# Stage 0 of a two-layer encoder trunk: radix-4 step, gate and convolution silu on PSUM operands, and GpSimd's squares behind the first product

## The chip, the cores and the metric

The kernel runs on one core of one Trainium2 chip. The core has five engines with a queue each: TensorE (PE in the profile, its weight loads PEld), VectorE (DVE), ScalarE (ACT), GpSimd (POOL) and SyncE (SP), which issues most DMAs. The metric is the device time of one execution in microseconds, as the median of several runs; lower is better. SBUF is the working memory; PSUM is the memory that matmuls write, in 8 banks of 128 partitions by 512 float32 values.

## The reference

The input x is (1, 1024, 1024) in float32: sequence by model width. Layer 0 normalizes, makes one input projection, sends 512 of its columns through mixer A (a real 2-D Fourier transform over sequence and head, then a map for each head) and 2 × 512 through mixer B (a gated convolution over 31 taps, a layer norm for each head, silu), joins both in an output projection and adds x. Layer 1 uses a pooling mixer. Each layer ends in a SwiGLU feed-forward block.

```python
h = rmsnorm(x, norm_mix_g[layer])
p = h @ w_in_ab[e]
ya = fnet_heads(p[..., :A_WIDTH], fnet_map[e])          # fft2 over sequence and head, real part, map
yb = conformer_conv_heads(p[..., A_WIDTH:A_WIDTH + B_WIDTH], p[..., A_WIDTH + B_WIDTH:], ...)
y = jnp.concatenate([ya, yb], axis=-1) @ w_out_ab[e]
x = x + y
h = rmsnorm(x, norm_ffn_g[layer])
x = x + (silu(h @ w_gate) * (h @ w_up)) @ w_down

# conformer_conv_heads
u = v * sigmoid(gate)
u = conv31(u) + conv_b
yb = silu(layernorm_per_head(u))
```

## The kernel before, in words

**Data and number format.** Everything is held transposed: channels on the 128 partitions, the sequence of 1024 along the free dimension, in two halves of 512 (`HALVES`). Each float32 operand of a matmul is split into a rounded high part and a low part (the residue), and a product is three matmuls (`mm3`, L101 to L103: high by high, high by low, low by high). `split` (L88, L89) makes the parts: a cast on ACT, then a subtraction on DVE or POOL.

**The order of work.** The source lists the work in one order. The framework's planner fixes the order on each engine when the program is built, by its own estimates of durations and by the source's order as priority, and it gives out buffers in that plan. So ACT's squares stand between casts that the source lists ahead of them. On the chip each engine then works through its queue strictly in that order. Buffers belong to tags with a fixed number of slots: `ps` has 4 PSUM banks, `lnp` has 2, `acc` is a pair of banks, `half` has 6 slots in SBUF. A product that finds no free `ps` bank waits for the instruction that reads the old one last.

**Pacing.** `mm3` keeps marks: after each three matmuls the number of columns that PE has streamed so far. `paced(ins, rows)` makes an instruction wait for the first mark at or over `rows`.

**The start.** Two weight tiles (value and gate columns of the first convolution head) and x arrive by DMA. `split_x` (L163, L164) makes high and low parts `gxh`, `gxl` of x times the norm's gain for each of 8 channel tiles and a half. `in_mm` forms a product of 8 `mm3` for 128 output columns and one half. The norm's sum of squares is shared: POOL squares tiles 0, 2, 4, 6 (`sq_pool`, L172 to L176), ACT squares the other four and DVE adds them (L131, L134, L135). `inv_x` adds the two sums (L187), a matmul with a constant matrix (L140) sums over channels, and `rsqrt2` (L123 to L126) makes the factor `invs[t]` that multiplies products when they are evacuated.

**The gate.** `vg_evac` (L214 to L217) evacuates the value product and the gate product with the factor into SBUF tiles `vt` and `g`, applies the sigmoid on ACT in place, and writes their product to `us[c]`, the input of the convolution.

**The convolution in the background.** Its 31 taps for each of 4 channel tiles run beside the products: tiles 1 and 2 on DVE (L313, L315, accumulating in the PSUM pair `acc`), tile 0 on ACT and POOL (L304 multiplies into `pr`, L305 adds), tile 3 on both (L330 on DVE). `tick(used)` is called after each product: it counts the columns that PE streamed since the last call, turns them into microseconds, subtracts `used` for the DVE work of that product, and emits as many steps of DVE's convolution stream as fit; POOL's taps are paced by columns. `conv_ln` (L343 to L355) is the layer norm over a head's 128 channels, with two matmuls, and the silu (L354), whose result is split (L88, L89).

**The radix-4 step.** For each of 4 Fourier heads, two products are evacuated into a tile `at` of 1024 columns (L426). A radix-4 butterfly on its four quarters q0 to q3 follows (L434 to L439): q0 + q2, q1 + q3, q0 − q2, q1 − q3, then the sum and the difference of the first two. `split` makes `zh`, `zl` of the tile (L440). Then `fnet1` (two `ps` banks a step, evacuated at L462 and L463) and `fnet2` (one bank, L482 and L483) run for 8 steps, followed by the output projection's Fourier half (`op_one`, L504), its convolution half, and the feed-forward blocks.

Of the kernel before, what the change touches and what calls it, by code (L numbers as in the profile page):

```python
# [12 lines left out]
AF = mybir.ActivationFunctionType  # L13
ALU = mybir.AluOpType
# [5 lines left out]
KD = D // P  # L20
FF = 2816
NF = FF // P
TH = 512
TAPS = 31
PAD = TAPS // 2
# [10 lines left out]
HALVES = (slice(0, TH), slice(TH, S))  # L36

V_MIX, V_FFN, V_FIN, V_CB, V_LG, V_LB, V_PS = 0, 16, 32, 40, 44, 48, 52
# [4 lines left out]
def trunk(ctx: ExitStack, tc: tile.TileContext, xT, vecs, cw, w_in, w_out, fmap, pmap,  # L43
          wg, wu, wd, wdq, wdp, cen_m, pcnt, dft_h, dft_l, seq_h, seq_l, out):
    nc = tc.nc
# [6 lines left out]
    def big(name, dt=F32, cols=1024):  # L52
        return arena.tile([P, WW], dt, tag="big", name=name, bufs=28)[:, :cols]

    def half(name, dt=F32):
        return arena.tile([P, TH], dt, tag="half", name=name, bufs=HALF_BUFS)

    def small(name, dt=F32):
        return arena.tile([P, TH], dt, tag="ln", name=name, bufs=4)

    def bank(tag="ps"):
        return psum.tile([P, TH], F32, tag=tag, name=tag, bufs=4 if tag == "ps" else 2)

    TT = nc.vector.tensor_tensor
# [3 lines left out]
    vec = const.tile([P, NV], F32, name="vec")  # L68
# [18 lines left out]
    def split(hi, lo, src, eng=None):  # L87
        nc.scalar.copy(hi, src)  # L88
        (eng or nc.vector).tensor_tensor(out=lo, in0=src, in1=hi.bitcast(F32), op=ALU.subtract)  # L89
# [3 lines left out]
    def paced(ins, rows):  # L93

        mark = next((m for n, m in marks if n >= rows), marks[-1][1])
        tc.add_manual_dep(ins.ins, mark.ins.name, mybir.DependencyInfo(
            mybir.DependencyClass.Sync, mybir.DependencyReason.DATA), reason="pace")

    def mm3(ps, lhs, rhs, start, stop, **kw):
        (lh, ll), (rh, rl) = lhs, rhs  # L100
        nc.tensor.matmul(ps, lh, rh, start=start, stop=False, **kw)  # L101
        nc.tensor.matmul(ps, lh, rl, start=False, stop=False, **kw)  # L102
        mm = nc.tensor.matmul(ps, ll, rh, start=False, stop=stop, **kw)  # L103
        marks.append((marks[-1][0] + 3 * ps.free_size(), mm))
# [13 lines left out]
    def wslice(w, i):  # L118
        return w[0][:, i * P:(i + 1) * P], w[1][:, i * P:(i + 1) * P]

    def rsqrt2(ps, e, y, v):

        nc.scalar.activation(y, ps, AF.Abs_reciprocal_sqrt, bias=eps[:, e:e + 1])  # L123
        STT(out=v, in0=ps, scalar=(RMS_EPS, LN_EPS)[e], in1=y, op0=ALU.add, op1=ALU.mult)
        TT(out=v, in0=v, in1=y, op=ALU.mult)
        STT(out=v, in0=v, scalar=-3.0, in1=y, op0=ALU.add, op1=ALU.mult)  # L126
        return v
# [25 lines left out]
    xin = [big(f"xin{k}") for k in range(KD)]  # L153
# [6 lines left out]
    def split_x(t, k):  # L160
        hs = HALVES[t]
        g = gneg[:, V_MIX + k:V_MIX + k + 1]
        nc.scalar.activation(gx_h[k][:, hs], xin[k][:, hs], AF.Copy, scale=g)  # L163
        STT(out=gx_l[k][:, hs], in0=xin[k][:, hs], scalar=g, in1=gx_h[k][:, hs].bitcast(F32),  # L164
            op0=ALU.mult, op1=ALU.subtract)

    def sq_pool(t, pooled):
        hs = HALVES[t]
        accp = half("accp")
        for k in pooled:  # L170
            if k == pooled[0]:
                nc.gpsimd.tensor_tensor(out=accp, in0=xin[k][:, hs], in1=xin[k][:, hs], op=ALU.mult)  # L172
            else:
                pr = arena.tile([P, TH], F32, tag="pr", name="pr", bufs=2)
                nc.gpsimd.tensor_tensor(out=pr, in0=xin[k][:, hs], in1=xin[k][:, hs], op=ALU.mult)
                nc.gpsimd.tensor_tensor(out=accp, in0=accp, in1=pr, op=ALU.add)  # L176
        return accp

    def sq_rest(t, pooled):
        acc = half("acc")  # L180
        rest = [k for k in range(KD) if k not in pooled]
        for k in rest:
            sq_acc(acc, xin[k][:, HALVES[t]], k == rest[0])
        return acc

    def inv_x(acc, accp):
        TT(out=acc, in0=acc, in1=accp, op=ALU.add)  # L187
        return inv_from(acc)

    def in_w(m, **kw):  # L190
        return load_w(w_in[m], **kw)

    def in_mm(w, t, ps=None):
        ps = bank() if ps is None else ps
        for k in range(KD):
            mm3(ps, wslice(w, k), (gx_h[k][:, HALVES[t]], gx_l[k][:, HALVES[t]]), k == 0, k == KD - 1)
        return ps

    invs = [None, None]
    us = [big(f"u{c}", cols=UW) for c in range(4)]  # L200
# [9 lines left out]
        vg_evac(c, t, in_mm(wv, t, pv), in_mm(wgt, t, pg))  # L210

    def vg_evac(c, t, pv, pg):
        vt, g = half("vt"), half("g")
        TT(out=vt, in0=pv, in1=invs[t], op=ALU.mult)  # L214
        TT(out=g, in0=pg, in1=invs[t], op=ALU.mult)
        nc.scalar.activation(g, g, AF.Sigmoid)
        TT(out=us[c][:, PAD + t * TH:PAD + (t + 1) * TH], in0=vt, in1=g, op=ALU.mult)  # L217

    def make_tables():

# [27 lines left out]
    for k in range(KD):  # L248
        if k % 4 == 0:
            hs = HALVES[k // 4]  # L250
# [5 lines left out]
    pv, pg = [in_mm(wv, 0)], [in_mm(wgt, 0)]  # L256
# [4 lines left out]
    df_h, df_l = df_hl[:, 0:2 * P], df_hl[:, 2 * P:4 * P]  # L261
    for dst, src in ((df_h, dft_h), (df_l, dft_l)):
        paced(nc.gpsimd.dma_start(dst, src), 1)
    accp = sq_pool(0, POOLED0)
    acc = sq_rest(0, POOLED0)
    for k in range(KD):
        split_x(1, k)
    invs[0] = inv_x(acc, accp)
    pv.append(in_mm(wv, 1))
    pg.append(in_mm(wgt, 1))  # L270
# [1 line left out]
    accp = sq_pool(1, POOLED1)  # L272
# [8 lines left out]
    yb_h, yb_l = [None] * 8, [None] * 8  # L281
# [54 lines left out]
    def conv_ln(c, alloc, ts=(0, 1)):  # L336
        if yb_h[4 + c] is None:
            yb_h[4 + c], yb_l[4 + c] = alloc(f"ybh{4 + c}", dt=F32R), alloc(f"ybl{4 + c}", dt=F32R)
        cv = {t: cvs[("p", c, t) if c == 0 else (c, t)] for t in ts}
        a, b = {t: small("lna") for t in ts}, {t: small("lnb") for t in ts}  # L340
        for t in ts:
            ps = bank("lnp")
            nc.tensor.matmul(ps, cen, cv[t], start=True, stop=True)  # L343
            nc.scalar.activation(a[t], ps, AF.Square)
            nc.scalar.copy(cv[t], ps)
        for t in ts:
            ps = bank("lnp")
            nc.tensor.matmul(ps, ones, a[t], start=True, stop=True)
            rsqrt2(ps, 1, a[t], b[t])
            TT(out=b[t], in0=cv[t], in1=b[t], op=ALU.mult)  # L350
            yield 2.4
        for t in ts:
            hs = HALVES[t]
            nc.scalar.activation(a[t], b[t], AF.Silu, bias=vec[:, V_LB + c:V_LB + c + 1],  # L354
                                 scale=gneg[:, V_LG + c:V_LG + c + 1])  # L355
            split(yb_h[4 + c][:, hs], yb_l[4 + c][:, hs], a[t])
            yield 0.6

    def dve_stream():
# [19 lines left out]
    def tick(used):  # L379

        rows = marks[-1][0]
        while behind["pool"] and behind["at"] <= rows:
            ins = next(behind["pool"], None)
            if ins is None:
                behind["pool"] = None
                break
            paced(ins, behind["at"])
            behind["at"] += 3800
        if behind["dve"]:
            behind["free"] += (rows - behind["last"]) / 2370.0 - used  # L390
            while behind["free"] > 0 and behind["dve"]:
                cost = next(behind["dve"], None)
                if cost is None:
                    behind["dve"] = None
                else:
                    behind["free"] -= cost
        behind["last"] = rows
# [16 lines left out]
    def load_seq(c):  # L414
        sq_h[c], sq_l[c] = big(f"sqh{c}", F32R), big(f"sql{c}", F32R)
        for dst, src in ((sq_h[c], seq_h[c]), (sq_l[c], seq_l[c])):
            paced(nc.gpsimd.dma_start(dst, src), marks[-1][0])
# [3 lines left out]
    z_h, z_l = [], []  # L421
    for h in range(4):
        w = in_w(h)
        at = big("at")
        for t in range(2):
            TT(out=at[:, HALVES[t]], in0=in_mm(w, t), in1=invs[t], op=ALU.mult)  # L426
            tick(2.8)

        zs = half("zs")
        z_h.append(big("zh", F32R))  # L430
        z_l.append(big("zl", F32R))
        q = [at[:, a * 256:(a + 1) * 256] for a in range(4)]
        z0, z1 = zs[:, 0:256], zs[:, 256:512]
        TT(out=z0, in0=q[0], in1=q[2], op=ALU.add)  # L434
        TT(out=z1, in0=q[1], in1=q[3], op=ALU.add)
        TT(out=q[0], in0=q[0], in1=q[2], op=ALU.subtract)
        TT(out=q[1], in0=q[1], in1=q[3], op=ALU.subtract)
        TT(out=q[2], in0=z0, in1=z1, op=ALU.add)
        TT(out=q[3], in0=z0, in1=z1, op=ALU.subtract)  # L439
        split(z_h[h], z_l[h], at)  # L440
    load_seq(2)
    load_seq(3)

# [62 lines left out]
    for mp in range(4):  # L506
        w = pool_w(w_out[mp])
# [588 lines left out]
```

## Time and profile before

| What | Value |
|---|---|
| median of 3 runs | 1733.5 us (1731.33 to 1737.66) |
| profiled execution | 1727.4 us |
| its span | 1725.6 us, 21770 instructions |
| busy: PE, DVE, ACT, POOL | 1656.9, 1215.0, 793.9, 349.4 us |
| stage 0 ends, feed-forward begins | near 316 us (the first L543 at 316.60) |

The profile shows one execution. The span is the time between the first and the last instruction; the 1.8 us beside it lie around them. A row of the timeline has its start, its duration, the engine, the line of the kernel, the operation, output and inputs by name, shapes, and in brackets the idle time before it with what ended it. A row of a wait list reads: who waited for whom, the sum in us, how many times, the longest. A row of windows gives busy time and number of instructions for each engine asked, PE's granted clock as a share, the DMA share and GB/s. A row of a tile gives shortest, median and longest duration in ns. A row of a group ends in busy time in us and the mean in ns.

### The profile page before, as it was taken

The page shows a single profiled execution, that of the slowest core. Times are in us where ns is not written, and L with a number is a line of the kernel's source. Part 1 is how long each engine was busy: PE and PEld are TensorE (multiplying, and loading weights), DVE is VectorE, ACT ScalarE, POOL GpSimd, SP SyncE. Part 2 cuts the span into 40 slices and gives each one's busy share as a digit, 9 for nine tenths or more (in the row PEclk, how much of TensorE's full clock was granted, in tenths as well). Part 3 has the DMA queues.
Part 4 walks back from the last instruction along what each step waited for, and adds up shares of the span by engine and source line. Part 5 has one row for each costly group of instructions (what it writes and reads, how often), then busy time and mean ns, then how long its engine had stood idle before and what let it go on. Part 6 is the DMA issues. An engine that isn't in the chain of part 4 may idle for free.

```text
span 1725.6 us, 21770 instructions
## 1 busy us (share of the span) xinstructions
PE 1656.9 (96%) x7790; PEld 1353.6 (78%) x7790; DVE 1215.0 (70%) x1727; ACT 793.9 (46%) x1283; POOL 349.4 (20%) x400
## 2 busy tenths in 40 slices
PE   6998789999999999999999998999999999999997
PEld 4786777777787787779998886777777778888877
DVE  8699997785455656555558877787767677656666
ACT  5555756474444444433334335454343435354443
POOL 4486764211100000000000001211212121204000
PEclk9999899999999999999999999999999999999999
DMA  5121311445633333346443434655767677886664
GB/s 188 49 98 38 126 70 37 165 165 195 243 113 127 116 124 129 120 131 195 132 137 103 155 102 145 216 176 195 232 220 237 209 239 255 278 276 189 201 194 131
DMA packets 101517, 278.23 MB, mean 161 GB/s; under 512 B 13088, under 2 KB 18464, under 8 KB 101408
## 3 DMA queue, kind: packets, MB, share of 16 engines
q1 hardware_dynamic: 77760, 203.16, 36.5%
q0 software_dynamic: 21344, 70.53, 11.7%
q10 hardware_dynamic: 2304, 3.15, 0.5%
q8 instruction: 61, 1.00, 0.2%
q14 instruction: 48, 0.39, 0.1%
HBM read 209.42 MB, written 67.37 MB: 160 GB/s over the span
## 4 chain that ended last, share of the span: by engine, by line
PE 71%; DVE 11%; issue 8%; DMA 6%; ACT 2%; POOL 1%; SPq 0%; POOLq 0%; DVEq 0%; ACTq 0%
PE ps L101 16%; PE ps L103 16%; PE ps L102 16%; PE lnp L101 7%; PE lnp L103 7%; PE lnp L102 7%; DMA p<-p 3%; DVE acc L315 2%; DVE acc L135 1%; DVE hl L89 1%; DMA xin<-in_xT 1%; DMA bT<-cv 1%; ACT x L701 1%; POOL sS L687 0%; ACT hl L88 0%
## 5 line engine op out<-in xcount | busy, mean ns | idle before, releaser
L101 PE MATMUL ps<-hl 128*128 128x512 f32 x704 | 274.9, 396 | 11.2 <-ACT x L701 8.3
L102 PE MATMUL ps<-hl 128*128 128x512 f32 x704 | 276.6, 393 | 0.0
L103 PE MATMUL ps<-hl 128*128 128x512 f32 x704 | 273.5, 394 | 0.0
L88 ACT CAST hl<-raw 128x512 fp32r<-128x512 f32 x264 | 159.7, 619 | 243.8 <-PE lnp L103 96.3
L89 DVE TENSOR_TENSOR hl<-raw,hl 128x512 fp32r<-128x512 f32 x264 | 179.0, 689 | 118.4 <-ACT hl L88 118.2
L88 ACT CAST wh<-raw 128x1024 fp32r<-128x1024 f32 (+4 forms) x147 | 127.9, 870 | 198.8 <-PE ps L102 88.2
L101 PE MATMUL lnp<-hl 128*128 128x512 f32 x528 | 211.7, 401 | 6.1 <-ACT x L701 5.1
L103 PE MATMUL lnp<-hl 128*128 128x512 f32 x528 | 208.2, 395 | 0.0
L102 PE MATMUL lnp<-hl 128*128 128x512 f32 x528 | 208.0, 394 | 0.0
L89 DVE TENSOR_TENSOR wl<-raw,wh 128x896 fp32r<-128x896 f32 (+4 forms) x135 | 136.3, 1012 | 61.0 <-ACT wh L88 50.3
L101 PEld LDWEIGHTS ps<-hl 128*128 128x128 f32 x704 | 132.2, 188 | 51.3 <-ACT x L701 15.2
L103 PEld LDWEIGHTS ps<-hl 128*128 128x128 f32 x704 | 132.2, 188 | 30.5
L102 PEld LDWEIGHTS ps<-hl 128*128 128x128 f32 x704 | 132.3, 188 | 29.1
L305 POOL TENSOR_TENSOR cvp<-cvp,pr 128x512 f32<-128x512 f32 x96 | 137.6, 1434 | 84.6 <-ACT pr L304 80.3
L101 PEld LDWEIGHTS lnp<-hl 128*128 128x128 f32 x528 | 99.5, 188 | 38.7 <-ACT x L701 12.5
L103 PEld LDWEIGHTS lnp<-hl 128*128 128x128 f32 x528 | 99.5, 188 | 23.0
L102 PEld LDWEIGHTS lnp<-hl 128*128 128x128 f32 x528 | 99.6, 189 | 22.2 <-issue 0.7
L101 PE MATMUL ps<-ahl,wh 128*128 128x504 f32 (+2 forms) x358 | 115.3, 322 | 0.0
L103 PE MATMUL ps<-ahl,wl 128*128 128x504 f32 (+2 forms) x358 | 114.8, 321 | 0.0
L102 PE MATMUL ps<-ahl,wh 128*128 128x504 f32 (+2 forms) x358 | 114.7, 320 | 0.0
L101 PE MATMUL ps<-hl,wh 128*128 128x512 f32 (+1 forms) x308 | 111.8, 363 | 0.0
L103 PE MATMUL ps<-hl,wl 128*128 128x512 f32 (+1 forms) x308 | 111.4, 362 | 0.0
(242 smaller groups left out, 3410.9 us busy)
## 6 DMA issues: line engine op xcount, KB each, us to landing
raw<-in_wg SPq DMA_DIRECT2D x66, 512.0 KB, 4.0
raw<-in_wu SPq DMA_DIRECT2D x66, 512.0 KB, 3.8
raw<-in_wd SPq DMA_DIRECT2D x32, 448.0 KB, 3.4
p<-s POOLq DMA_DIRECT2D x44, 256.0 KB, 3.1
p<-p SPq DMA_DIRECT2D x44, 256.0 KB, 4.7
a<-g POOLq DMA_DIRECT2D x44, 256.0 KB, 2.8
q<-in_wdq SPq DMA_DIRECT2D x44, 256.0 KB, 6.2
sS<-q POOLq DMA_DIRECT2D x44, 256.0 KB, 4.6
```

Source lines behind the costliest of these rows:

```text
L88: nc.scalar.copy(hi, src)
L89: (eng or nc.vector).tensor_tensor(out=lo, in0=src, in1=hi.bitcast(F32), op=ALU.subtract)
L101: nc.tensor.matmul(ps, lh, rh, start=start, stop=False, **kw)
L102: nc.tensor.matmul(ps, lh, rl, start=False, stop=False, **kw)
L103: mm = nc.tensor.matmul(ps, ll, rh, start=False, stop=stop, **kw)
L135: TT(out=acc, in0=acc, in1=sq, op=ALU.add)
L305: nc.gpsimd.tensor_tensor(out=a, in0=a, in1=pr, op=ALU.add)
L315: STT(out=acc, in0=src, scalar=wv, in1=acc, op0=ALU.mult, op1=ALU.add)
L701: nc.scalar.copy(x, bd)
```

## The change

Four edits, all in layer 0.

- **POOL's squares.** The first square of half 0 waits for the mark at 12000 columns. In the source, the splits of half 1 of x (`split_x(1, k)`) now stand ahead of the squares of half 0 instead of behind them.
- **Gate.** The tile `g` is gone: the scaled gate is written back to its PSUM bank, the sigmoid works in that bank, and the last product reads one operand from PSUM and `vt` from SBUF.
- **Convolution silu.** The silu writes into the `lnp` bank of the second matmul instead of an SBUF tile, and the split reads it from there.
- **Radix-4 step.** The tile `at` is gone. Both products are scaled in place in their `ps` banks. ACT copies the second one to SBUF (`zs`), then DVE forms sum and difference with 512 columns each, in place in the banks; ACT copies a quarter again, and DVE forms the last difference and sum. The split is done in two halves from the banks. The `used` of the tick goes from 2.8 to 2.6.

```diff
@@ sq_pool
-                nc.gpsimd.tensor_tensor(out=accp, in0=xin[k][:, hs], in1=xin[k][:, hs], op=ALU.mult)
+                ins = nc.gpsimd.tensor_tensor(out=accp, in0=xin[k][:, hs], in1=xin[k][:, hs], op=ALU.mult)
+                if t == 0:
+                    paced(ins, 12000)
@@ vg_evac
-        vt, g = half("vt"), half("g")
+        vt = half("vt")
         TT(out=vt, in0=pv, in1=invs[t], op=ALU.mult)
-        TT(out=g, in0=pg, in1=invs[t], op=ALU.mult)
-        nc.scalar.activation(g, g, AF.Sigmoid)
-        TT(out=us[c][:, PAD + t * TH:PAD + (t + 1) * TH], in0=vt, in1=g, op=ALU.mult)
+        TT(out=pg, in0=pg, in1=invs[t], op=ALU.mult)
+        nc.scalar.activation(pg, pg, AF.Sigmoid)
+        TT(out=us[c][:, PAD + t * TH:PAD + (t + 1) * TH], in0=pg, in1=vt, op=ALU.mult)
@@ start
+    for k in range(KD):
+        split_x(1, k)
     accp = sq_pool(0, POOLED0)
     acc = sq_rest(0, POOLED0)
-    for k in range(KD):
-        split_x(1, k)
     invs[0] = inv_x(acc, accp)
@@ conv_ln
-        a, b = {t: small("lna") for t in ts}, {t: small("lnb") for t in ts}
+        a, b, ln = {t: small("lna") for t in ts}, {t: small("lnb") for t in ts}, {}
...
-            ps = bank("lnp")
+            ps = ln[t] = bank("lnp")
...
-            nc.scalar.activation(a[t], b[t], AF.Silu, bias=vec[:, V_LB + c:V_LB + c + 1],
+            nc.scalar.activation(ln[t], b[t], AF.Silu, bias=vec[:, V_LB + c:V_LB + c + 1],
                                  scale=gneg[:, V_LG + c:V_LG + c + 1])
-            split(yb_h[4 + c][:, hs], yb_l[4 + c][:, hs], a[t])
+            split(yb_h[4 + c][:, hs], yb_l[4 + c][:, hs], ln[t])
@@ heads
-        at = big("at")
+
+        q = []
         for t in range(2):
-            TT(out=at[:, HALVES[t]], in0=in_mm(w, t), in1=invs[t], op=ALU.mult)
-            tick(2.8)
-
+            q.append(in_mm(w, t))
+            TT(out=q[t], in0=q[t], in1=invs[t], op=ALU.mult)
+            tick(2.6)
         zs = half("zs")
...
-        q = [at[:, a * 256:(a + 1) * 256] for a in range(4)]
-        z0, z1 = zs[:, 0:256], zs[:, 256:512]
-        TT(out=z0, in0=q[0], in1=q[2], op=ALU.add)
-        TT(out=z1, in0=q[1], in1=q[3], op=ALU.add)
-        TT(out=q[0], in0=q[0], in1=q[2], op=ALU.subtract)
-        TT(out=q[1], in0=q[1], in1=q[3], op=ALU.subtract)
-        TT(out=q[2], in0=z0, in1=z1, op=ALU.add)
-        TT(out=q[3], in0=z0, in1=z1, op=ALU.subtract)
-        split(z_h[h], z_l[h], at)
+        nc.scalar.copy(zs, q[1])
+        TT(out=q[1], in0=q[0], in1=zs, op=ALU.add)
+        TT(out=q[0], in0=q[0], in1=zs, op=ALU.subtract)
+        split(z_h[h][:, HALVES[0]], z_l[h][:, HALVES[0]], q[0])
+        z0, z1 = q[1][:, 0:256], zs[:, 0:256]
+        nc.scalar.copy(z1, q[1][:, 256:512])
+        TT(out=q[1][:, 256:512], in0=z0, in1=z1, op=ALU.subtract)
+        TT(out=z0, in0=z0, in1=z1, op=ALU.add)
+        split(z_h[h][:, HALVES[1]], z_l[h][:, HALVES[1]], q[1])
```

## The prediction

> **What bounds the kernel now.** I read the page first: the span, the busy shares, the slices of TensorE (PE).
>
> ```profile
> span 1725.6 us, 21770 instructions
> PE 1656.9 (96%) x7790; PEld 1353.6 (78%) x7790; DVE 1215.0 (70%) x1727; ACT 793.9 (46%) x1283; POOL 349.4 (20%) x400
> ...
> PE   6998789999999999999999998999999999999997
> ```
>
> PE is busy for 96% of the span and idle for 68.7 us (1725.6 − 1656.9). The slices, 43 us each, put most of that idle time into the first seven, which is the part the change edits. So I asked for the busy time by stages (PE, weight loads, VectorE = DVE, ScalarE = ACT, GpSimd = POOL, granted clock, DMA) and for what PE waited for.
>
> ```profile
> 166.40:200.00 33.60, 22.09 (x134) 19.34 (x133) 31.72 (x37) 22.36 (x33) 19.29 (x16) 0.80 0.22 80
> 200.00:240.00 40.00, 33.94 (x237) 30.92 (x236) 39.20 (x38) 30.37 (x43) 27.11 (x19) 0.96 0.37 132
> 240.00:283.00 43.00, 43.00 (x180) 33.48 (x179) 36.48 (x49) 22.43 (x31) 29.59 (x19) 1.00 0.12 38
> ...
> 350.00:1725.00 1375.00, 1346.59 (x6403) 1108.12 (x6401) 914.33 (x1385) 593.79 (x998) 150.94 (x246) 1.00 0.54 177
> ```
>
> ```profile
> PE ps L101 <- DVE at L426: 8.9, 1, 8.9
> PE ps L101 <- DVE wcl L463: 2.5, 1, 2.5
> PE lnp L343 <- DVE cv L320: 1.3, 1, 1.3
> ```
>
> After 350 PE runs at 98% of the time (1346.59 of 1375) on work that the change leaves alone, so what PE gains or loses before then reaches the end whole. From 166 to 240 DVE is the engine that is full (31.72 of 33.60, 39.20 of 40) and PE waits for it: 8.9 us for the evacuations at L426, 2.5 us for the Fourier residues at L463, 6.1 us in all from 200 to 240 (40 − 33.94).
>
> Next comes the start, in the timeline, with the residue gxl of the input by its tile.
>
> ```profile
> 9.58 1.22 PE L101 MATMUL ps<-gxh,wh 128*128 128x512 f32 x2 [9.58 <-ACT gxh L163]
> ...
> 27.76 0.63 PE L102 MATMUL ps<-gxl,wh 128*128 128x512 f32 x1
> 28.19 0.63 PE L103 MATMUL ps<-gxh,wl 128*128 128x512 f32 x1
> ...
> 35.90 0.40 PE L103 MATMUL ps<-gxh,wl 128*128 128x512 f32 x1
> 36.13 1.02 PE L140 MATMUL lnp<-acc,onesd 128*128 128x512 f32 x2
> ```
>
> ```profile
> L164 DVE SCALAR_TENSOR_TENSOR gxl<-xin,gneg,gxh x16: 739/1132/1768, 10.3 to 34.5; 128x512 fp32r<-128x512 f32 x16
> L175 POOL TENSOR_TENSOR pr<-xin x6: 1039/1298/1486, 8.8 to 26.9; 128x512 f32<-128x512 f32 x6
> ...
> PEld ps L102 <- DVE gxl L164: 11.0, 8, 3.0
> ```
>
> Two products of 24 matmuls take PE from 9.58 to 36.13, 26.5 us. Matmuls start 0.43 us apart there (27.76, 28.19) and 0.23 apart once PE runs without gaps (35.90, 36.13). The weight loads stand 11.0 us in front of gxl, whose instructions take 0.74 us at best and 1.77 at worst: all have two SBUF operands, and the long ones lie beside POOL's squares.
>
> **Part 1: POOL's squares behind the first product.** POOL's first square waits for the product's last matmul (8 steps of 3 × 512 rows = 12288, the first mark over 12000). Queued behind it on POOL are the other 13 squares and sums only; the next work is far off:
>
> ```profile
> 28.49 1.61 POOL L176 TENSOR_TENSOR accp<-accp,pr 128x512 f32<-128x512 f32 x1
> 59.00 1.29 POOL L305 TENSOR_TENSOR cvp<-cvp,pr 128x512 f32<-128x512 f32 x1 [28.90 <-ACT pr L304]
> ```
>
> That gap of 28.9 us takes the delay. Without POOL beside them, 8 residues at 0.74 and 4 weight residues at about the same need 8.9 us, less than the product itself when it is slow (24 × 0.43 = 10.3). So the first product ends near 9.58 + 10.3 = 19.9 and the second, 24 × 0.23 = 5.6, near 25.5: 10.6 us earlier than 36.13. What is late next is the normalizer: 4 squares at 1.30 and 3 sums at 1.61 from 19.9 make 30.0, the add on DVE (about 0.7) 30.7, and its matmul at L140 sits behind the second product on PE, in front of the third. There PE would wait 5.2 us; the order on an engine is the planner's, so the matmul may also be placed inside the third product and cost nothing. At the other end DVE, now doing 8 residues of the second half (moved ahead of the sums) beside POOL at 1.49 (POOL's longest square) plus 3 sums, is free only at 18.5 + 11 × 1.49 = 34.9 and past the add at 35.6: a wait of 10.1, with a slow clock after it, leaves nothing of the gain. Bounds 0 and 10.6; I take **6.0**, a little over the value with the matmul in its old place (5.4), since both orders are possible.
>
> **Part 2: the radix-4 step on PSUM.** The prices, for DVE, then ACT:
>
> ```profile
> 120.00:176.50 56.50, 27.84 (x27) 3.15 (x3) 0.97 0.20 69
> L426 DVE TENSOR_TENSOR at<-ps,v x8: 675/678/685, 123.3 to 178.6; 128x512 f32<-128x512 f32 x8
> L434 DVE TENSOR_TENSOR zs<-at x4: 411/1708/2625, 129.0 to 183.2; 128x256 f32<-128x256 f32 x4
> ...
> L439 DVE TENSOR_TENSOR at<-zs x4: 408/410/410, 134.0 to 184.9; 128x256 f32<-128x256 f32 x4
> ...
> L217 DVE TENSOR_TENSOR u<-vt,g x8: 684/891/1433, 53.2 to 119.0; 128x512 f32<-128x512 f32 x8
> ```
>
> ```profile
> L462 ACT CAST wch<-ps 128x512 fp32r<-128x512 f32 x16 | 9.5, 591 | 0.4 <-PE ps L102 0.4
> ...
> L231 ACT CAST tbh<-ps 128x256 fp32r<-128x256 f32 x4 | 1.4, 372 | 2.4 <-PE ps L103 2.4
> ```
>
> The first row is the time of DVE and ACT on the tile `at` alone, heads 0 to 2. L434, with two SBUF operands, ranges from 0.41 to 2.63 us for 256 columns; L426, one operand in PSUM, is 0.68 every time for twice the columns. Of the 27.84 us, 6 evacuations at 0.68 stay; 23.8 go. In their place each head has four instructions of 512 columns (add, subtract, two low parts) and two of 256, all with one PSUM operand: 4 × 0.68 + 2 × 0.41 = 3.5, for three heads 10.6. DVE saves 13.2 us before head 3's evacuations. A PSUM output is not in these rows; the conv taps write PSUM, and I add nothing. ACT gains two copies (0.59 + 0.37) and casts in two pieces of 0.59 instead of one of 3.15 / 3 = 1.05: +1.1 a head, while ACT is busy 22.36 of 33.60.
>
> How late DVE is at that point:
>
> ```profile
> 166.12 0.39 PE L103 MATMUL ps<-gxh,wl 128*128 128x512 f32 x1
> ...
> 168.38 0.28 PE L103 MATMUL ps<-tbh,zl 128*128 128x256 f32 x1
> 177.60 0.55 PE L101 MATMUL ps<-tbh,zh 128*128 128x256 f32 x1 [8.94 <-DVE at L426]
> 177.95 0.42 PE L102 MATMUL ps<-tbl,zh 128*128 128x256 f32 x1
> 178.17 0.41 PE L103 MATMUL ps<-tbh,zl 128*128 128x256 f32 x1
> ...
> 188.66 0.41 PE L102 MATMUL ps<-sql,wch 128*128 128x256 f32 x1
> ...
> 178.57 0.68 DVE L426 TENSOR_TENSOR at<-ps,v 128x512 f32<-128x512 f32 x1
> ```
>
> Head 3's last product ends near 166.4 and is evacuated at 178.57: 12.2 late. The 13.2 saved, less 8 × 0.2 = 1.6 us of conv taps that the smaller tick lets in, plus some 1.7 us at L217 (8 × (0.89 − 0.68), 0.89 its median), cancel it. What replaces the wait: a bank is now free only when its butterfly and low part are done. From the last product: evacuate 0.68, copy 0.59, add 0.68, subtract 0.68, two of 256 columns 0.82, cast 0.59, low part 0.68 = 4.7; the first Fourier step covers 2.1 (166.35 to 168.4), so PE waits 2.6, or 6.6 with two conv taps (about 1.3) and two ACT taps (0.7) in between. I take 4.6. Slow matmuls behind the old wait start 0.22 apart instead of 0.12 (0.28 long at 168.38, 0.42 at 177.95); with 32 of them up to 188.7 that was 3.2 us. Before: 8.9 + 2.5 + 3.2 = 14.6. After: 4.6 + 2.0 of slow clock = 6.6. Gain **8.0**, bounds 12.0 (wait 2.6, no slow clock) and −5 (a rival below).
>
> On the clock, this row decides the 2.0:
>
> ```profile
> 288.00 1.44 PE L343 MATMUL lnp<-cv,cen 128*128 128x512 f32 x2 [2.29 <-DVE cv L333]
> ...
> 289.66 0.63 PE L101 MATMUL ps<-ybh,wh 128*128 128x512 f32 x1
> 290.08 0.63 PE L102 MATMUL ps<-ybl,wh 128*128 128x512 f32 x1
> ```
>
> Here 2.29 us of idle PE were enough for starts 0.42 apart (289.66, 290.08). [...]
>
> **Part 3: gate, silu, Fourier stage.**
>
> ```profile
> L89 DVE TENSOR_TENSOR ybl<-lna,ybh 128x512 fp32r<-128x512 f32 x4 | 7.1, 1801 | 0.0
> ```
>
> From 200 to 240 PE lost 6.1 us to a late DVE. The low parts of the convolution's silu, now from PSUM, fall from 1.80 to 0.68, 4.5 us for the four before 250, so DVE stays on time; I count half of the 6.1: **3.0**, bounds 0 and 6. The wait of 1.3 at L343 sits behind head 0's butterflies: **1.0**. The gate keeps its bank through sigmoid and product, some 2 us (an estimate, two instructions like L217's), against the 11.0 of the next pair of products (48 × 0.23): nothing. The tail (cv at L333, 2.29) I leave: from 240 to 283 DVE (36.48) and POOL (29.59) have room to follow an earlier PE; bounds 3 better, 5 worse.
>
> **Sum.** 6.0 + 8.0 + 3.0 + 1.0 = 18.0. The profiled execution took 1727.4 us, 6.1 below the median of 1733.5: 1709.4 on its scale, **1715.5** as a median.
>
> **Rivals.**
> - *Full recovery*: normalizer's matmul moved, short bank wait: 10.6 + 12.0 + 6.0 + 1.0 = 29.6, 1704. For it: nothing but the planner's order stands in the way at the start. Against: DVE and ACT hold conv taps in between.
> - *The waits move from the port to ACT*: DVE now depends on ACT four times a head instead of once, and ACT's taps wait for POOL:
>
> ```profile
> ACT pr L304 <- POOL cvp L305: 11.2, 12, 1.9
> ```
>
>   At the mean of 0.93 a hop, 16 hops make 15 us, the whole saving on DVE. Only parts 1 and the 1.0 stay: 1726.5. Against: the planner can put taps into such gaps.
> - *Banks held too long, slower*: with the longest wait, 1.9, at four hops and a tap of 1.3 in front of four DVE steps, the chain is 4.7 + 7.6 + 5.2 = 17.5. It decides from 11.0 us on (the 48 matmuls of the next head that cover it). Heads 2, 3 and the first Fourier step then wait 6.5 each, 19.5, and the second 15.4 instead of 14.6; less the 7.0 of part 1 and L343 that is +13.3: 1747. [...] Against: only one old wait on PE in this stretch was for a bank.
>
> **How the numbers follow.** Likeliest 0.56 (own range 1706 to 1723), full recovery 0.16, moved waits 0.18, banks 0.10. I call 0.5%, 8.7 us, what can be told from no change. Faster 0.75: the likeliest, the full recovery and a small part of the third; same 0.15: the rest of the third and the likeliest's edge; slower 0.10: the banks. Range 1700 to 1731 leaves out the banks case and the far half of the full recovery.
>
> **What would show it.** L164 near 0.74 for the first eight and the matmul of 36.13 near 25 to 31 (part 1); time on PE in front of L140 (the normalizer); L434's successors at 0.41 to 0.68 with POOL running, head 3 evacuated within 2 us of its product, PE's wait before the second Fourier step under 7 us (part 2); idle PE from there to the output projection under 4 us (part 3). Wrong if DVE shows waits on ACT of a few us per head, or if PE waits inside the heads' products.

## The result and the profile after

The changed kernel took 1712.5 us as a median, against 1732.4 us for the kernel before; the ratio is 0.988, with a 95% interval from 0.985 to 0.990. It is faster by 19.9 us; the prediction said 18.0 less, 1715.5 us. One of its executions ran at a granted clock of 0.752 from end to end and took 2027.5 us, and the profile fell on that one, so the profile after is taken from a second measurement of the same kernel (1709.5 us, ratio 0.987, interval 0.985 to 0.989, beside a kernel before of 1731.7). The page of that execution begins:

```profile
span 1709.3 us, 21772 instructions
PE 1649.0 (96%) x7790; PEld 1347.2 (79%) x7790; DVE 1191.0 (70%) x1723; ACT 796.1 (47%) x1295; POOL 343.1 (20%) x400
```

DVE's work fell by 24.0 us (1215.0 − 1191.0); the prediction's savings for three of the four heads, the gate and the silu make 19.4 (13.2 + 1.7 + 4.5). ACT's work rose by 2.2 us, half of the 1.1 a head that was predicted. What PE gained is better read up to a fixed instruction than from the span, since the rest of the execution scatters: behind the mark used here, it took between 1376.6 and 1385.0 us over the profiles of twelve kernels, with no order that follows the edits. The mark is the first matmul of the feed-forward that waits for its copy `s`. A mark is read from the one profiled execution of a kernel, so it has no interval. These are that row in the timeline and PE's, the weight loads', DVE's, ACT's and POOL's busy time from 36.10 to it, for the kernel before:

```profile
348.06 0.50 PE L101 MATMUL ps<-hl 128*128 128x512 f32 x1 [1.62 <-ACT s L617]
...
36.10:348.06 311.96, 287.40 (x1327) 230.79 (x1326) 270.66 (x312) 179.45 (x254) 176.40 (x125) 0.97 0.26 87
```

and for the changed kernel:

```profile
328.93 0.50 PE L101 MATMUL ps<-hl 128*128 128x512 f32 x1 [1.69 <-ACT s L620]
...
36.10:328.93 292.83, 280.56 (x1320) 224.62 (x1318) 252.40 (x306) 180.80 (x265) 173.75 (x129) 0.99 0.27 92
```

The mark comes 19.1 us earlier (348.06 − 328.93). PE's idle time in the stretch fell from 24.6 us (311.96 − 287.40) to 12.3, and its busy time by 6.8 us for 7 matmuls fewer. Seven matmuls at 0.23 us are 1.6; the other 5.2 are matmuls that no longer run at the slow clock. The granted clock agrees: in this stretch PE was busy for 15.4 us at a clock of 0.50 in the kernel before and for 5.9 in the changed one, and half of the difference is 4.8.

The timeline of PE in the changed kernel, at the start:

```profile
32.82 2.08 PE L140 MATMUL lnp<-acc,onesd 128*128 128x512 f32 x2 [5.58 <-DVE acc L189]
...
35.12 0.63 PE L102 MATMUL ps<-gxl,wh 128*128 128x512 f32 x1
35.55 0.63 PE L103 MATMUL ps<-gxh,wl 128*128 128x512 f32 x1
...
45.50 1.02 PE L140 MATMUL lnp<-acc,onesd 128*128 128x512 f32 x2
```

PE came to the matmul at L140 at 27.24 (32.82 − 5.58), behind 57 matmuls; the kernel before came to it at 36.13, behind 54, so the same work was done some 9.6 us earlier (8.9, and 3 × 0.23). Then the normalizer's matmul held PE for 5.6 us and left it slow: matmuls start 0.43 apart (35.12, 35.55). The second matmul at L140, behind 96 matmuls of products in both kernels, came at 45.50 against 46.69 before, so 1.2 of the 9.6 us were left.

From the heads to the tail:

```profile
162.86 0.40 PE L103 MATMUL ps<-gxh,wl 128*128 128x512 f32 x1
165.63 0.39 PE L101 MATMUL ps<-tbh,zh 128*128 128x256 f32 x1 [2.37 <-DVE zl L89]
165.85 0.28 PE L102 MATMUL ps<-tbl,zh 128*128 128x256 f32 x1
165.97 0.28 PE L103 MATMUL ps<-tbh,zl 128*128 128x256 f32 x1
...
169.66 0.39 PE L101 MATMUL ps<-tbh,zh 128*128 128x256 f32 x1 [2.19 <-DVE zl L89]
...
173.97 1.12 PE L345 MATMUL lnp<-cvp,cen 128*128 128x512 f32 x2 [2.62 <-POOL cvp L307]
...
270.62 1.10 PE L345 MATMUL lnp<-cv,cen 128*128 128x512 f32 x2 [0.88 <-DVE cv L335]
```

The wait of 8.94 us at 177.60 is gone, and so is the one for the Fourier residues (2.50). Two waits for a bank have come, 2.37 + 2.19 = 4.56 us, and a wait of 2.62 us for POOL's convolution taps of tile 0, which an earlier PE now reaches before they are done. Matmuls behind the first bank wait start 0.12 apart (165.85, 165.97): no slow clock there. It came behind the wait for the taps: from 175.09 to 178.50 the granted clock was 0.50. The tail's wait at `cv` fell from 2.29 to 0.88.

What DVE paid for the new steps, by line and by tile (shortest, median and longest in ns):

```profile
L436 DVE TENSOR_TENSOR ps<-ps,zs x4: 684/688/700, 128.2 to 171.4; 128x512 f32<-128x512 f32 x4
L441 DVE TENSOR_TENSOR ps<-ps,zs x4: 412/422/423, 131.6 to 177.3; 128x256 f32<-128x256 f32 x4
L89 DVE TENSOR_TENSOR zl<-ps,zh x8: 673/691/692, 131.0 to 181.1; 128x512 fp32r<-128x512 f32 x8
L219 DVE TENSOR_TENSOR u<-ps,vt x7: 680/684/692, 49.1 to 117.7; 128x512 f32<-128x512 f32 x7
```

With one operand in PSUM each took the same time every time, to 0.02 us, with POOL at work beside it; writing PSUM (L436) cost nothing over writing SBUF (L219).

Why PE still waits for the banks shows in ACT's timeline ahead of the first of the two:

```profile
161.52 0.72 ACT L306 ACTIVATE pr<-u,cwt 128x512 f32<-128x512 f32 x1 [3.86 <-POOL cvp L307]
162.26 1.28 ACT L356 ACT_TABLE_LOAD   x1
163.56 0.78 ACT L356 ACTIVATE lnp<-lnb,vec,gneg 128x512 f32<-128x512 f32 x1
164.28 0.57 ACT L88 CAST zh<-ps 128x512 fp32r<-128x512 f32 x1
```

and in DVE's, and in DVE's list of waits from 100 to 200:

```profile
164.89 0.69 DVE L89 TENSOR_TENSOR zl<-ps,zh 128x512 fp32r<-128x512 f32 x1 [1.55 <-ACT zh L88]
...
169.52 0.69 DVE L430 TENSOR_TENSOR ps<-ps,v 128x512 f32<-128x512 f32 x1
...
DVE zl L89 <- ACT zh L88: 6.7, 6, 2.2
```

ACT stood 3.86 us at a tap that needed a `pr` slot from POOL, loaded a table, did the silu, and only then cast `zh`. DVE's residue waited for the cast, and PE for the residue's bank. The row at 169.52 is the evacuation of head 3's second half.

### The profile page after: what moved, and what is told of

The parts are those of the page before. It is cut to its first block, busy times and chain, and to the rows that moved or that the text cites. A ratio compares the mean times of both kernels' runs of the same rounds, so it can differ in the third digit from the quotient of the medians.

```text
span 2025.7 us, 21772 instructions
## 1 busy us (share of the span) xinstructions
PE 1995.6 (99%) x7790; PEld 1458.6 (72%) x7790; DVE 1200.8 (59%) x1723; ACT 802.1 (40%) x1295; POOL 339.5 (17%) x400
## 4 chain that ended last, share of the span: by engine, by line
PE 97%; DVE 1%; POOL 1%; DMA 1%; issue 1%; ACT 0%; SPq 0%; POOLq 0%; DVEq 0%; ACTq 0%
PE ps L101 22%; PE ps L103 22%; PE ps L102 22%; PE lnp L102 10%; PE lnp L101 10%; PE lnp L103 10%; DMA xin<-in_xT 1%; PE lnp L350 0%; PE lnp L345 0%; PE lnp L546 0%; DVE acc L135 0%; PE acc L102 0%; PE acc L101 0%; POOL accp L178 0%; PE acc L103 0%
## 5 line engine op out<-in xcount | busy, mean ns | idle before, releaser
L102 PE MATMUL ps<-hl 128*128 128x512 f32 x704 | 321.0, 456 | 0.0
L101 PE MATMUL ps<-hl 128*128 128x512 f32 x704 | 316.7, 456 | 1.2 <-ACT s L620 1.2
L103 PE MATMUL ps<-hl 128*128 128x512 f32 x704 | 317.7, 457 | 0.0
L101 PE MATMUL lnp<-hl 128*128 128x512 f32 x528 | 242.5, 460 | 1.4 <-ACT s L620 0.7
L102 PE MATMUL lnp<-hl 128*128 128x512 f32 x528 | 242.1, 458 | 0.0
L103 PE MATMUL lnp<-hl 128*128 128x512 f32 x528 | 240.9, 456 | 0.0
L101 PEld LDWEIGHTS ps<-hl 128*128 128x128 f32 x704 | 139.8, 199 | 61.8 <-ACT s L620 1.8
L102 PEld LDWEIGHTS ps<-hl 128*128 128x128 f32 x704 | 140.1, 199 | 59.4
L103 PEld LDWEIGHTS ps<-hl 128*128 128x128 f32 x704 | 139.5, 198 | 59.9
L307 POOL TENSOR_TENSOR cvp<-cvp,pr 128x512 f32<-128x512 f32 x96 | 128.4, 1338 | 100.6 <-ACT pr L306 99.0
L101 PEld LDWEIGHTS lnp<-hl 128*128 128x128 f32 x528 | 105.4, 200 | 48.8 <-ACT s L620 1.7
L102 PEld LDWEIGHTS lnp<-hl 128*128 128x128 f32 x528 | 104.9, 199 | 45.3 <-issue 1.2
L103 PEld LDWEIGHTS lnp<-hl 128*128 128x128 f32 x528 | 105.3, 199 | 44.6
L101 PE MATMUL ps<-ahl,wh 128*128 128x504 f32 (+2 forms) x358 | 131.1, 366 | 0.0
L102 PE MATMUL ps<-ahl,wh 128*128 128x504 f32 (+2 forms) x358 | 129.6, 362 | 0.0
L103 PE MATMUL ps<-ahl,wl 128*128 128x504 f32 (+2 forms) x358 | 129.5, 362 | 0.0
L101 PE MATMUL ps<-hl,wh 128*128 128x512 f32 (+1 forms) x308 | 128.4, 417 | 0.0
L102 PE MATMUL ps<-hl,wh 128*128 128x512 f32 (+1 forms) x308 | 128.4, 417 | 0.0
```

The source lines that it names most:

```text
L307: nc.gpsimd.tensor_tensor(out=a, in0=a, in1=pr, op=ALU.add)
```

## The experiments

All were run in three groups, each beside the kernel before on the same chip, the first group on one chip and the other two on a second; the median of the kernel before was 1731.7, 1730.6 and 1730.9 us. "Mark" is the matmul above, at 348.06 in the kernel before and at 328.93 in the changed kernel.

### The changed kernel again

> The whole change once more, for a profile at full clock. Theory A (the parts add: an earlier first product, plus a VectorE that is on time in the heads): about 20 us under the kernel before, near 1712; the matmul that closes the norm near 25 to 31 us, head 3's second product evacuated within 2 us of its end, PE idle from the first Fourier step to the output projection under 5 us. Theory B (only the start gains, the waits in the middle come back elsewhere): the same time, but with 10 us or more of idle PE between 150 and 230.

1709.5 us, ratio 0.987 (0.985 to 0.989). The gain is there again, and its rows were shown above. The time is that of theory A, but two of its signs in the middle are missing: the second half of head 3 was evacuated at 169.52, 6.4 us after its product ended near 163.1, and PE was idle for 6.5 us between the first Fourier step (165.63) and the output projection (218.75). Between 150 and 230 it was idle for 9.6 us, just under the 10 that theory B asked for.

### The start alone

```diff
-                nc.gpsimd.tensor_tensor(out=accp, in0=xin[k][:, hs], in1=xin[k][:, hs], op=ALU.mult)
+                ins = nc.gpsimd.tensor_tensor(out=accp, in0=xin[k][:, hs], in1=xin[k][:, hs], op=ALU.mult)
+                if t == 0:
+                    paced(ins, 12000)
...
+    for k in range(KD):
+        split_x(1, k)
     accp = sq_pool(0, POOLED0)
     acc = sq_rest(0, POOLED0)
-    for k in range(KD):
-        split_x(1, k)
```

> Only GpSimd's wait and the moved splits; gate, silu and radix-4 step as before. Theory A: 6 to 9 us under before (1723 to 1726), and the wait of 8.9 us before the second Fourier step is still there, some 8 us earlier. Theory B: 15 us or more under before (under 1717).

1730.2 us, ratio 0.999 (0.998 to 1.000): no gain that can be told, and less than either expectation. PE's timeline in this kernel:

```profile
32.73 2.07 PE L140 MATMUL lnp<-acc,onesd 128*128 128x512 f32 x2 [5.00 <-DVE acc L189]
...
174.91 0.55 PE L101 MATMUL ps<-tbh,zh 128*128 128x256 f32 x1 [7.83 <-ACT ybh L88]
184.01 0.39 PE L101 MATMUL ps<-sqh,wch 128*128 128x256 f32 x1 [4.05 <-DVE wcl L465]
...
346.58 0.50 PE L101 MATMUL ps<-hl 128*128 128x512 f32 x1 [1.74 <-ACT s L619]
```

The same wait at L140 with the same slow matmul behind it; the mark is 1.5 us earlier. What is left of the gain at the start meets a DVE that is as late as before: the two waits at the heads come to 11.9 us (7.83 + 4.05), against 11.4 before.

### The radix-4 step alone

The edit is the last hunk of the diff (the two products stay in their banks, the butterfly works on them, `tick(2.6)`), with nothing else.

> Only the radix-4 step on PSUM with its tick of 2.6; the start, gate and silu as before. Theory A: 8 to 12 us under before (1720 to 1724), first two products unchanged (closing matmul near 36 us), VectorE's instructions of the step at 0.41 to 0.75 us. Theory B: within 3 us of before, because the new waits of VectorE on ScalarE or of PE on banks take the saved time.

1715.5 us, ratio 0.991 (0.989 to 0.993): 16 us, more than either expectation. Windows and timeline of this kernel:

```profile
36.10:331.08 294.98, 282.58 (x1327) 227.09 (x1326) 249.08 (x308) 180.49 (x264) 172.71 (x125) 0.99 0.27 92
...
173.58 1.12 PE L343 MATMUL lnp<-cvp,cen 128*128 128x512 f32 x2 [3.97 <-POOL cvp L305]
```

The mark came 17.0 us earlier (348.06 − 331.08). PE did the same 1327 matmuls with 12.2 us less idle time (24.6 to 12.4) and 4.8 us less busy time (287.40 − 282.58, the slow clock). DVE's busy time fell by 21.6 us. So this part alone takes the idle time to what the whole change leaves, 12.3, and the wait for POOL's taps belongs to it.

### The gate and the silu, together and singly

The two edits on PSUM operands, with the radix-4 step and the start as before:

```diff
-        vt, g = half("vt"), half("g")
+        vt = half("vt")
...
-        TT(out=g, in0=pg, in1=invs[t], op=ALU.mult)
-        nc.scalar.activation(g, g, AF.Sigmoid)
-        TT(out=us[c][:, PAD + t * TH:PAD + (t + 1) * TH], in0=vt, in1=g, op=ALU.mult)
+        TT(out=pg, in0=pg, in1=invs[t], op=ALU.mult)
+        nc.scalar.activation(pg, pg, AF.Sigmoid)
+        TT(out=us[c][:, PAD + t * TH:PAD + (t + 1) * TH], in0=pg, in1=vt, op=ALU.mult)
...
-            nc.scalar.activation(a[t], b[t], AF.Silu, bias=vec[:, V_LB + c:V_LB + c + 1],
+            nc.scalar.activation(ln[t], b[t], AF.Silu, bias=vec[:, V_LB + c:V_LB + c + 1],
...
-            split(yb_h[4 + c][:, hs], yb_l[4 + c][:, hs], a[t])
+            split(yb_h[4 + c][:, hs], yb_l[4 + c][:, hs], ln[t])
```

> Only the gate and the convolution silu on PSUM operands. Theory A: 1 to 4 us under before (1728 to 1731): 8 gate products and 8 low parts become 0.3 to 1.1 us shorter, and VectorE is full from 75 to 240 us. Theory B: no difference that can be measured.

1720.4 us, ratio 0.994 (0.992 to 0.996), 11.2 us by the medians: above the expectation too. Then the silu alone (the last two changes of that diff):

> Only the convolution silu on PSUM. If the gain of gate and silu (11 us) comes from the four low parts of 1.8 us that become 0.7 in the middle of the Fourier stage: 6 to 10 us under before (1722 to 1726). If it comes from the gate, whose eight products stand where VectorE begins to be late: under 3 us.

1724.0 us, ratio 0.996 (0.995 to 0.998), 6.6 us, in the range given for the low parts. And the gate alone (the first three):

> The gate's product and sigmoid on PSUM alone, everything else as before. The silu alone took 7.6 us off the median of before in one measurement and gate and silu together 10.2. Theory overlap (each edit only makes VectorE less late at head 3, so that the parts add as long as together they stay under the 12.2 us of lateness): 2 to 4 us, 1726.5 to 1728.5. Rival (each edit recovers most of what there is to recover alone, and the two together little more): 6 to 8 us, 1722.5 to 1724.5.

1724.4 us, ratio 0.996 (0.995 to 0.998), 6.5 us, by the rival. The windows up to the mark, for gate and silu together:

```profile
36.10:336.77 300.67, 284.83 (x1329) 227.37 (x1327) 262.47 (x313) 178.30 (x254) 172.09 (x125) 0.98 0.27 91
```

for the silu:

```profile
36.10:340.45 304.35, 285.85 (x1328) 230.83 (x1326) 263.64 (x312) 176.68 (x252) 176.71 (x125) 0.97 0.26 90
```

and for the gate:

```profile
36.10:340.41 304.31, 284.29 (x1328) 227.22 (x1327) 265.68 (x312) 178.75 (x254) 174.27 (x125) 0.98 0.27 90
```

The marks are 11.3, 7.6 and 7.7 us earlier. The two edits that bring 7.6 and 7.7 singly bring 11.3 together: already here the parts do not add. So the silu's 6.6 us do not show that the gain of both comes from the low parts, as its expectation would read them: the gate brings as much by itself.

### All but the start

The changed kernel with the first two hunks undone: radix-4 step, gate and silu.

> Radix-4 step, gate and silu on PSUM operands, the start as before. Theory S: 1 to 3 us over the whole change (1710 to 1713), since the start brought about 1.5 us net. Theory T: equal to the whole change. If the parts simply added (radix 16, gate and silu 11): 27 us under before, 1704.

1714.1 us, ratio 0.990 (0.988 to 0.992). The windows of this kernel:

```profile
36.10:330.97 294.87, 283.39 (x1328) 226.75 (x1326) 250.91 (x308) 181.63 (x266) 168.71 (x125) 0.98 0.27 93
```

The time is just outside what theory S gave it (1710 to 1713); simple adding, 1704, is out. The mark stands at 330.97, that of the radix-4 step alone at 331.08: gate and silu, worth 11.3 us by themselves, add 0.1 on top of it at the mark, and about 1 us by the ratios (0.990 against 0.991), whose intervals overlap. The parts pay one debt, the lateness of DVE, and the radix-4 step alone pays nearly all that they pay together. The start adds 2.0 us more at the mark (330.97 − 328.93). By the ratios it adds some 5 us (0.990 against 0.987, of 1731), but these are from two groups and two chips, and their intervals overlap, so it is left at 2 to 5.

### The normalizer's add behind the second half's products

```diff
-    invs[0] = inv_x(acc, accp)
     pv.append(in_mm(wv, 1))
     pg.append(in_mm(wgt, 1))
+    invs[0] = inv_x(acc, accp)
```

in the changed kernel, so that the planner puts the matmul at L140 later in PE's order.

> The whole change with one line moved: the first norm factor is computed behind the second half's two products, so the matmul that closes the norm (L140) stands behind 96 matmuls on TensorE instead of 57. Theory S (the start's gain was lost in the wait of 5.6 us at that matmul and the slow clock behind it): the wait is gone, the second L140's products end about 7 us earlier than in the whole change, and the time is 5 to 8 us under it (1702 to 1705). Theory T (the gain of the start is lost again anyway, because VectorE or GpSimd bound the middle): the start is as early, but the time is within 2 us of the whole change.

1706.4 us, ratio 0.985 (0.983 to 0.988). PE's timeline:

```profile
36.41 1.02 PE L140 MATMUL lnp<-acc,onesd 128*128 128x512 f32 x2
44.71 0.50 PE L103 MATMUL acc<-gxh,wl 128*128 128x512 f32 x1 [1.21 <-DVE wl L89]
...
159.50 0.39 PE L101 MATMUL ps<-tbh,zh 128*128 128x256 f32 x1 [2.85 <-DVE zl L89]
...
323.11 0.50 PE L101 MATMUL ps<-hl 128*128 128x512 f32 x1 [1.61 <-ACT s L620]
```

No wait at L140 and no slow matmul, and every later stage is earlier by about as much: the first Fourier step 6.1 us (165.63 − 159.50), the mark 5.8 us (328.93 − 323.11). So once DVE is on time, time saved at the start does reach the end; what took it away in the changed kernel was the place of this matmul. In the medians the step is some 3 us, less than the 5 to 8 of theory S and more than theory T allowed, and the two intervals overlap; that it beats the kernel before is clear, that it beats the changed kernel rests on the traces.

### All of POOL's squares behind the first product

The same kernel, and the wait also on the squares into `pr`:

```diff
-                nc.gpsimd.tensor_tensor(out=pr, in0=xin[k][:, hs], in1=xin[k][:, hs], op=ALU.mult)
+                ins = nc.gpsimd.tensor_tensor(out=pr, in0=xin[k][:, hs], in1=xin[k][:, hs], op=ALU.mult)
+                if t == 0:
+                    paced(ins, 12000)
```

The reason is in the changed kernel's timelines of POOL, of DVE, and of POOL again:

```profile
8.69 1.04 POOL L177 TENSOR_TENSOR pr<-xin 128x512 f32<-128x512 f32 x1 [7.55 <-DMA xin<-in_xT]
...
8.81 1.47 DVE L89 TENSOR_TENSOR wl<-raw,wh 128x512 fp32r<-128x512 f32 x1 [2.19 <-ACT wh L88]
...
21.77 3.23 POOL L172 TENSOR_TENSOR accp<-xin 128x512 f32<-128x512 f32 x1 [7.99 <-PE ps L103]
```

Only the square into `accp` has the wait, and the planner put two others ahead of it, this one and the next at 10.74; a weight residue beside them took 1.47 us.

> The changed kernel with the add of the normalizer moved behind the second half's products, and now all of GpSimd's squares of the first half waiting for the first product, where two ran ahead before. Theory start (squares beside VectorE's residues still cost the first two products): residues of the weights at 0.7 instead of 1.5 us, the first product about 1 to 2 us shorter, 1704 to 1705.5 against 1706.4. Rival (the products are short enough, and the normalizer that now comes later is what costs): 1706.5 to 1709.

1707.7 us, ratio 0.988 (0.985 to 0.990): nothing more, by the rival. The rows of this kernel, of DVE, POOL and then PE:

```profile
8.98 0.69 DVE L89 TENSOR_TENSOR wl<-raw,wh 128x512 fp32r<-128x512 f32 x1 [1.72 <-ACT wh L88]
...
20.76 3.23 POOL L172 TENSOR_TENSOR accp<-xin 128x512 f32<-128x512 f32 x1 [7.53 <-PE ps L103]
...
45.85 0.50 PE L103 MATMUL acc<-gxh,wl 128*128 128x512 f32 x1 [3.12 <-DVE wl L89]
```

The residue fell to 0.69, and the first product, which releases POOL, was through 1.0 us earlier than in the changed kernel (21.77 − 20.76). It came back as a wait of 3.12 us for a later weight residue on DVE. The mark, at 323.28, did not move.

### Without POOL's taps, before and after

POOL's 96 additions of the convolution's taps are taken out, of the kernel before and of the changed kernel:

```diff
-                        nc.gpsimd.tensor_tensor(out=a, in0=a, in1=pr, op=ALU.add)
```

> The kernel before without GpSimd's additions of the background convolution (96 instructions left out, so tiles 0 and 3 miss taps); VectorE's instructions are all as before. [...]

> The changed kernel without GpSimd's 96 adds of the convolution taps of tiles 0 and 3, so these tiles lack those taps (the output is not the reference's). The same removal took the kernel before from 1731 to 1703.7. Theory port (the change freed most of what GpSimd's reads took from VectorE; what is left is the wait of 2.6 us for GpSimd's taps and some slower steps): 3 to 8 us, 1701 to 1706. Rival (GpSimd still costs as much as before, now by ScalarE waiting behind it): 20 us or more, under 1690.

The kernel before took 1703.7 us in one execution without them, 27 us less; the changed kernel 1700.5 us, ratio 0.982 (0.981 to 0.984), 9 us less than the changed kernel by the ratios (0.982 against 0.987), a little more than theory port gave it and far from the rival's 20. So without the taps the whole change is worth some 3 us (1703.7 − 1700.5, one execution against four), and with them 22.2 (1731.7 − 1709.5): most of what it brings is relief from POOL.

One line less stands in this kernel, so that L434 of the kernel before, the first instruction of the old butterfly, is L433 here. This is its tile row, and then its longest instruction and what POOL did beside it:

```profile
L433 DVE TENSOR_TENSOR zs<-at x4: 416/418/2624, 129.0 to 167.6; 128x256 f32<-128x256 f32 x4
...
142.80 2.62 DVE L433 TENSOR_TENSOR zs<-at 128x256 f32<-128x256 f32 x1
...
142.70 2.44 POOL L89 TENSOR_TENSOR wl<-raw,wh 128x1024 fp32r<-128x1024 f32 x1 [23.48 <-ACT wh L88]
```

Of the butterfly's 24 instructions, which ran up to 2.63 us in the kernel before, 23 took 0.41 to 0.42 with the same operands in SBUF. The 24th took 2.62: it ran beside work still left to POOL, a weight residue from 142.70 to 145.14, and ended 0.28 us after it. So two operands in SBUF were not slow by themselves here; POOL at work beside them stretched them. By what way was not shown: "the port", in the title of a rival and in the name of a theory, is the author's word for it. The tile `at` cost DVE 17.6 us before head 3's evacuations, against 27.84 in the kernel before, and PE's wait of 8.9 us was gone. What the changed kernel still pays, by the windows without POOL's taps:

```profile
36.10:317.44 281.34, 277.38 (x1318) 223.02 (x1316) 243.89 (x305) 179.99 (x264) 43.14 (x33) 1.00 0.28 95
...
DVE zl L89 <- ACT zh L88: 1.6, 3, 0.7
```

PE's idle time falls from 12.3 to 4.0 us, and DVE's wait for the cast, from 100 to 200, from 6.7 to 1.6. The row of 3.86 us above names how: POOL holds ACT. This run takes away POOL's waits and its work beside DVE's at once, so the share of each in the 8.3 us is not separated by it. A third `pr` slot, which would separate them, was not tried.

## Why the prediction was right, and where it was not

The sum was right (18.0 predicted, 19.1 at the mark, 19.9 in the medians), its division was not, so that the closeness of the sum is in part luck. By four rows of PE that both traces have (the last matmul of head 3's products, the Fourier step behind the old wait, the wait for `cv` in the tail, the mark):

| Stretch, ending at (before, after) | Predicted gain | Measured |
|---|---|---|
| head 3's products (166.12, 162.86) | 7.0: start 6.0, L343 1.0 | 3.3 |
| the second Fourier step (177.60, 169.66) | 4.3: 8.9 − 4.6 | 4.7 (7.9 − 3.3) |
| the wait for `cv` (288.00, 270.62) | 6.7: 2.5, clock 1.2, Fourier 3.0 | 9.4 (17.4 − 7.9, rounded) |
| the mark (348.06, 328.93) | 0 | 1.7 |

**The start, 6.0.** The mechanism was right: residues at 0.74, products out of the way by 27.24 (25.5 predicted, for 48 matmuls; 57 stand in front of the wait), then a wait at L140 of 5.58 (5.2 predicted, for the matmul in its old place). "Two products of 24 matmuls take PE from 9.58 to 36.13" was misread by a little: 54 matmuls stand there. The matmul itself came at 32.82, outside the 25 to 31 that was to show this part. The step that failed is "I take 6.0, a little over the value with the matmul in its old place": a slow clock was put behind the wait only in the worst case. It was there with the ordinary wait, with a granted clock of 0.50 from 31.73 to 38.55, and of 9.6 us 1.2 were left, 1.5 at the mark in the kernel with the start alone. Moving the matmul brought 5.8 us back, so that the upper bound had its condition right, the matmul's place; its 10.6 us were not reached. "Queued behind it on POOL are the other 13 squares and sums only" failed as well: two squares ran in front of the paced one in the changed kernel, at no cost that the run without them could show.

**The L343 wait, 1.0.** It came: the waits of 1.32 us at L343 and of 0.41 us at L348 behind head 0's butterflies are gone.

**The radix-4 step, 8.0.** The prices were right to 0.02 us. The bank wait of 4.6 us was met by 4.56, by luck: it came as two waits, one of them in front of the first Fourier step, and not by the chain worked out for it: that chain was butterfly steps and taps, and the trace shows ACT held by POOL ahead of the cast. "Head 3 evacuated within 2 us of its product" fell: it was 6.4 us, about half of the 12.2 before. The term was under-sized because the gain of an earlier DVE was counted at the heads only, and what it does to the Fourier stage, the slow clock and the tail was given to part 3 or to nothing. Alone, the step brought 17.0 us at the mark. The slow clock is the clearest size that was off: 1.2 us (3.2 − 2.0) predicted, 4.8 measured with the same number of matmuls. By the granted clock the kernel before lost 7.7 us to it (half of 15.4), in four stretches; the 3.2 were for the first two, and those from 234.01 and 288.62, 1.7 us each, were left out. The 2.0 allowed for the change came nearly right in size and not in place: the stretch from 175.09 to 178.50 costs 1.7 us, behind the wait for the taps and not behind a bank wait. The lower bound of −5 for this term does not follow from the rival that it names, whose figures make −20.3 (14.6 − 19.5 − 15.4); no run came near either.

**Gate, silu and Fourier stage, 3.0.** As a term of its own it does not exist in the changed kernel: 11.3 us alone, 0.1 on top of the radix-4 step. The prediction added savings of DVE in three parts as if each had its own PE time to give back. They had one between them, and the sum came out because it was kept near that.

**The rivals.** The moved waits are in the trace in part: DVE waits 6.7 us for ACT, and ACT's longest wait for POOL rose from 1.9 to 3.9. They cost some of the gain, not all of it. The full recovery fell on the normalizer's matmul and on the taps. With 6.7 us for four heads DVE's waits for ACT stay under the few us a head that were to show the forecast wrong; the idle time of PE from the second Fourier step to the output projection, 4.3 us (from 169.66 to 218.75), is a little over its 4. The held banks did not come: no wait stands inside the heads' products. A wait that no case had is the 2.62 us for POOL's taps at L345, a part of the same shift: PE is earlier, POOL is not.

## What to carry to other kernels

Several edits that relieve one late engine share one gain: price the lateness once, as the wait it causes, the slow clock behind it and the stages after it, and then ask how much of it each edit covers, rather than adding up what each saves. When the gain is made, look at who is late next (here POOL, through ACT's casts), and at where the planner puts the one instruction that needs the slow side's result: moving one line of source brought more at the mark than the whole edit at the start.

## What was not expected of the hardware

In these traces the length of one idle stretch of PE did not decide its clock afterwards. In the kernel before, matmuls started 0.42 apart behind 2.29 us of idle time at 288.00. In the kernel with the gate alone the same pair came behind a wait as long, 2.30 us, and the granted clock behind it stayed at 1.00:

```profile
282.04 1.10 PE L343 MATMUL lnp<-cv,cen 128*128 128x512 f32 x2 [2.30 <-DVE cv L333]
```

Windows show the clock behind both waits, and behind the changed kernel's wait for POOL's taps (the first number behind the comma is PE's busy time, the third from the end the clock). For the kernel before, the gate alone and the changed kernel:

```profile
285.21:288.62 3.41, 1.12 (x5) 0.41 (x3) 3.27 (x6) 1.56 (x2) 0.91 (x1) 1.00 0.42 127
288.62:292.04 3.42, 3.42 (x9) 2.35 (x8) 1.94 (x3) 1.07 (x2) 0.00 (x0) 0.50 0.07 26
...
280.89:284.30 3.41, 2.26 (x8) 1.60 (x9) 3.20 (x6) 1.08 (x2) 0.00 (x0) 1.00 0.49 154
284.30:287.72 3.42, 3.42 (x14) 2.46 (x14) 1.22 (x3) 1.59 (x2) 0.00 (x0) 1.00 0.00 0
...
171.68:175.09 3.41, 1.12 (x3) 0.65 (x4) 2.85 (x4) 0.70 (x2) 3.41 (x5) 1.00 0.38 118
175.09:178.50 3.41, 3.41 (x6) 1.25 (x6) 1.78 (x4) 3.35 (x6) 0.92 (x2) 0.50 0.97 299
```

In the kernel before, PE was idle for 2.29 us in the first window (3.41 − 1.12); the next 3.42 us ran at 0.50, with 9 matmuls. With the gate alone the wait lies from 279.74 to 282.04, 1.15 us of it in the first window (3.41 − 2.26); both windows ran at 1.00, the second with 14 matmuls in 3.42 us. In the changed kernel 2.29 us of idle time in the first window were followed by 3.41 us at 0.50. These are three waits; what decides the clock behind a wait is not shown by them, and no run varied the idle time on purpose.

So a wait of 2.29 us was followed by a stretch of 3.42 us at 0.50 in one profile, and one of 2.30 us by none in another. Such a stretch costs 1.7 us of busy time (an estimate, half of 3.42), and two marks that differ by 1 or 2 us should not be told apart by that difference alone.
